# Two index-query projections as one more seven-product pair, with earlier token sums and a one-pass Silu

## The chip, the cores and the metric

The kernel runs on one core of a Trainium2 chip. The metric is the device time of one execution in microseconds. The parts of the core that appear below are TensorE (PE, matrix products; PEld is its loading of weights), VectorE (DVE, elementwise work), ScalarE (ACT, functions and copies), GpSimd (POOL) and SyncE (SP, which issues most loads). Data lies in SBUF (128 partitions); matrix products land in PSUM banks and are taken out by ACT or DVE.

## The reference

One layer of a hybrid encoder on 512 tokens plus 16 learned meta tokens, width 2048, all in float32. The input is normalised and multiplied by one wide matrix whose columns are cut into parts:

```python
h = rms_norm(x, norm_g)
proj = h @ w_in                                   # [528, 2048] @ [2048, 12368]
(q_a, k_a, v_a, z_a, q_i, k_i, w_i,
 q_b, f_b, i_b, z_b, gates) = jnp.split(proj, cuts, axis=-1)
qi = apply_partial_rope(q_i.reshape(B, T, H_IDX, D_IDX), *rope_i)   # 16 heads of 64
...
score = jnp.einsum('bqhs,bqh->bqs', jax.nn.relu(idx_logits), wib)   # token indexer
_, sel = lax.top_k(score, topk)                   # 128 keys for each query
...
y_a = o_a * jax.nn.silu(z_a)                      # attention over the selected keys
y_b = o_b * jax.nn.silu(z_b)                      # gated linear recurrence
merged = jnp.sum(jax.nn.sigmoid(gates) * p, axis=2)
return x + merged @ w_out
```

Three parts matter here: q_i, the 1024 columns of index queries (eight blocks of 128 columns, two heads each), and z_a and z_b, the two gate paths of 1024 columns each that go through silu(z) = z * sigmoid(z).

## The kernel before

**Numbers in two halves.** Each float32 operand is split into a high half (fp32r, by an ACT copy) and a low half (the rest, by a DVE subtraction), and a product is three matmuls: high by high, high by low, low by high. The tokens lie as `hH[k]`, `hL[k]` for k = 0 to 15 (128 channels by 528 tokens each), the weights as `wh`, `wl`, three buffers of each in rotation.

**Plain jobs and pairs.** The projection is a list of jobs (L1794 on). A plain job (`Job`) takes 128 columns of the matrix, 16 blocks of channels, 512 tokens: 48 matmuls of 512 tokens. A `Pair` takes two blocks of 128 columns and computes them with seven products in place of eight (the Winograd form of Strassen's scheme): the channels are cut into two halves of eight blocks, the tokens into two halves of 256 (or 264 with the meta tokens). Its seven products `SEVEN` (L1506) are 24 matmuls each, `run_pair` (L1517) issues them. For the weights a pair needs four sums of raw chunks (`sum_1`, `sum_2` on DVE, `sum_3`, `sum_4` as accumulating DMAs on POOL's queue) and seven splits; for the results it combines the products in four PSUM banks called x, y, z and w (the tiles `px`, `py`, `pz`, `pw`) into two tiles g1 and g2, one for each block of columns. Before, the plain jobs are job 0 (index keys), jobs 1 to 8 (index queries) and jobs 9 and 10 (two blocks of z_b); the pairs follow: three of z_b, four of z_a, then keys with values, queries, gates and the recurrence's inputs, 43 in all. For the plain jobs the low half of a weight chunk is made by an ACT copy with scale -1 and an accumulating DMA (`hi_lo`, L430: preparations 8 to 21).

**Token sums.** The pairs need sums of the tokens' blocks too: `tops_task` (L1462) makes for each k from 0 to 7 the sums t1 and t2 (tile `tT`, high and low halves), t3 (kept in a shared slot until `place_t3`, L1494, writes it over a part of `hH[k]` and `hL[k]` that no later product reads otherwise) and t4 (one more tile `tT`, both halves in it). Two such tasks are spawned ahead of job 3 (`pre_t`, L1783, L1797). The first pair uses t2 in product 1, t3 in product 3, t1 in product 4 and t4 in product 5, counted from 0.

**Index tasks.** When a job of index queries is done, `idx_task` (L677) rotates it (DVE: a shuffle, two products, a sum), splits it into two tiles `qst`, and for each of its two heads issues ten matmuls into `psc`, lets ACT take them out with Relu, and adds them to the four score tiles with DVE. After the eighth of them the top-k tasks begin (`topk_task`, L752); attention needs their result after the last pair.

**Gate paths.** `silu` (L1406) and `silu_mul` (L1348) compute z * sigmoid(z): a Sigmoid on ACT, then a multiplication on DVE into a new slot, which is stored to DRAM by `spill`.

**What sets the order.** The program is written out by hand-made planning: the class `Core` keeps an estimated clock for each engine; `pump` is called after each block of channels and steps waiting tasks in order of their priority (a lower number first), as long as the estimated clocks of DVE and ACT are not too far ahead. A task that yields `WAIT` is asked again later; that moves its instructions in the order of the program. The engines run their queues in that order and wait for each other by semaphores.

**Slots.** SBUF beside the weights is 70 slots of 128 by 528 numbers (`Slots`). A slot's number modulo 4 is its place modulo 256 bytes, and the tiles that PE reads ask for a given residue (`home`). `main_slot` (L1509) steps tasks until a slot is free; `room` holds token tasks back while few are free.

Of the kernel before, what the change touches and what calls it, by code (L numbers as in the profile page):

```python
# [151 lines left out]
class Slots:  # L152
# [40 lines left out]

    def add(self, tags):
# [7 lines left out]
def hybrid_kernel(ctx, tc, x, meta, vecs, w_in, rows, w_branch, w_out,  # L202
# [117 lines left out]
    tabs = slots("tabs", 1)  # L320
    tabA = tabs[0][:, 0:320].rearrange("p (b d) -> p b d", b=5)
    RB = tabs[0][:, 320:512]
# [4 lines left out]
    def load_consts():  # L327
        nc.sync.dma_start(RB, rows.to_broadcast([128, 192]))
# [3 lines left out]
        nc.sync.dma_start(tabA, tab_a)  # L332
# [79 lines left out]
    def hi_lo(k, src, m, o, shift=0, turn=None):  # L412
# [17 lines left out]
        if 8 <= k < 22:  # L430
# [85 lines left out]
    def consts():  # L516
        yield E.clk["pe"] + 3000.0
# [17 lines left out]
        S.put(tabs[0])  # L535
# [85 lines left out]
    def ki_task(kw):  # L621
# [22 lines left out]
        E.tt(y, y, RB[:, None, 0:64].to_broadcast([128, 5, 64]), OP.mult)  # L644
# [30 lines left out]
    idx_left = [8]  # L675

    def idx_task(j, xq):  # L677
        a, b = slot("qpx"), slot("qxc")
# [6 lines left out]
        S.put(a, xq)  # L685
# [5 lines left out]
        S.put(b)  # L691
        yield e
# [6 lines left out]
        for i in range(2):  # L699
# [29 lines left out]
        S.put(*st_)  # L729
        idx_left[0] -= 1  # L730
# [110 lines left out]
    def tokens(src, x, d, tab, name):  # L841
# [12 lines left out]
        yield from room(1, 3)  # L854
# [24 lines left out]
    def ka_task(g, xk):  # L879
        y = yield from tokens({(0, 256): xk[:, 8:264], (2, 256): xk[:, 272:528]}, xk, kd_[g][:, 16:528],  # L880
                              "k", "ka")
        yield from room(1)
# [76 lines left out]
    def q_task(h, xq):  # L959
        y = yield from tokens({(0, 512): xq[:, :512]}, xq, qd_[h], "q", "qa")  # L960
        yield from room(1)
# [410 lines left out]
    def d_qi(j):  # L1372
        def f(b):
            s = slot("xqi")
# [70 lines left out]
    def d_zb(h):  # L1445
        def f(b):
            s = silu_mul(b, "hz")
            hg.setdefault(h, {})["z"] = 1
            spawn(spill(zd[h], s, E.clk["dve"] + LAT), 0)
# [10 lines left out]
    TB = {}  # L1460

    def tops_task(i):  # L1462
# [3 lines left out]
        for k in range(4 * i, 4 * i + 4):  # L1466
            while len(S.free) < (min(10, 6 + idx_left[0]) if idx_left[0] else 6) or k > 3 and k - 4 not in TB:
                yield WAIT
            if k % 2 == 0:
                t3 = slot("t3")  # L1470
            r1, r2, t1 = slots("tr", 3)
            c = r2
            d = t3[:, 264 * (k % 2):264 * (k % 2) + 264]
            E.tt(r1[:, al], hH[k][:, al].bitcast(F32), hL[k][:, al].bitcast(F32), OP.add)
            yield E.tt(r2[:, al], hH[8 + k][:, al].bitcast(F32), hL[8 + k][:, al].bitcast(F32), OP.add)
            E.tt(t1[:, lo], r1[:, lo], r1[:, hi], OP.subtract)
            E.tt(t1[:, hi], t1[:, lo], r2[:, hi], OP.add)
            E.tt(d, r1[:, hi], r2[:, hi], OP.subtract)
            e = E.tt(c[:, lo], r2[:, lo], t1[:, hi], OP.subtract)
            S.put(r1)  # L1480
            yield e
            a, b, t4 = slots("tT", 2, F32R, HC) + [slot("tT", F32R, HD)]
            E.act(a[:, al], t1[:, al], AF.Copy)
            E.act(t4[:, lo], c[:, lo], AF.Copy)
            E.tt(b[:, al], t1[:, al], a[:, al].bitcast(F32), OP.subtract)
            e = E.tt(t4[:, hi], c[:, lo], t4[:, lo].bitcast(F32), OP.subtract)
            S.put(t1, c)
            TB[k] = {"11": (hH[k][:, lo], hL[k][:, lo]), "t3": (hH[k][:, hi], hL[k][:, hi]),
                     "21": (hH[8 + k][:, lo], hL[8 + k][:, lo]), "22": (hH[8 + k][:, hi], hL[8 + k][:, hi]),
                     "t1": (a[:, lo], b[:, lo]), "t2": (a[:, hi], b[:, hi]), "t4": (t4[:, lo], t4[:, hi]),  # L1490
                     "tiles": (a, b, t4), "t3f": d, "t3s": t3}
            yield e

    def place_t3(k):  # L1494
# [4 lines left out]
        h, l = TB[k]["t3"]  # L1499
# [559 lines left out]
```

## Time and profile before

| | |
|---|---|
| median of 3 runs | 1464.0 us (1463.54 to 1464.99) |
| the profiled execution | 1463.6 us, of which 1461.6 us are its span, from the first to the last instruction |
| granted TensorE clock | 1.000 |
| PE busy | 1444.5 us (99%) |
| DVE busy | 1184.5 us (81%) |
| ACT busy | 715.6 us (49%) |
| POOL busy | 271.1 us (19%) |
| DMA | 263.35 MB, mean 180 GB/s |

Times in the profile are counted from the first instruction of the span. The start, with the norm and job 0 and 1, runs to about 50 us; the other plain jobs to 174 us; the pairs to 1081 us; then come the branch products with attention between them, and from 1301 us the last projection. A row of the profile names the line, the engine, the operation, and the tiles (out<-in); a line can be that of a helper, such as L107 for every ACT function and L114 for every DVE operation on two tensors.

### The profile page before, as it was taken

The numbers are of one execution on the slowest core, as the hardware profiler recorded it, in microseconds if no ns is written. First come the engines' busy times: TensorE is split into PE (matmuls) and PEld (weight loads), VectorE is DVE, ScalarE is ACT, GpSimd is POOL, SyncE is SP. The second block draws the span as 40 slices with busy tenths as digits, with TensorE's granted clock in tenths as the row PEclk, the third lists the DMA queues.
The fourth block names the chain that finished last, engine by engine and source line by source line (L and its number), as shares of the span: only waits on it lengthen the run. The fifth ranks groups of instructions, "written<-read, shape, count | busy, mean of one in ns | idle before, by whom it ended". The sixth has DMA issues, their size and how long they took to land.

```text
span 1461.6 us, 33043 instructions
## 1 busy us (share of the span) xinstructions
PE 1444.5 (99%) x13312; PEld 1408.9 (96%) x13312; DVE 1184.5 (81%) x2019; ACT 715.6 (49%) x1172; POOL 271.1 (19%) x346
## 2 busy tenths in 40 slices
PE   7999999999999999999999999999999999999999
PEld 6888899999999999999999999999999999999998
DVE  6699799999999988878877887888675666877676
ACT  5577644543545544444444444444466763334333
POOL 2201000002223310000001011000337410102222
PEclk9999999999999999999999999999999999999999
DMA  9266677778788987778777687868887434458873
GB/s 278 74 157 138 153 182 192 189 185 200 203 205 229 249 196 175 167 173 194 168 191 179 167 195 174 188 143 195 207 267 189 136 111 128 147 143 215 216 210 97
DMA packets 336072, 263.35 MB, mean 180 GB/s; under 512 B 32484, under 2 KB 303408, under 8 KB 335920
## 3 DMA queue, kind: packets, MB, share of 16 engines
q1 hardware_dynamic: 306160, 174.51, 41.9%
q0 software_dynamic: 24256, 80.45, 28.5%
q10 hardware_dynamic: 5504, 6.29, 1.3%
q8 instruction: 104, 1.70, 0.5%
q14 instruction: 48, 0.39, 0.1%
HBM read 170.40 MB, written 29.98 MB: 137 GB/s over the span
## 4 chain that ended last, share of the span: by engine, by line
PE 91%; DVE 4%; DMA 2%; issue 1%; ACT 1%; POOL 0%; SPq 0%; DVEq 0%; ACTq 0%; POOLq 0%
PE px L97 15%; PE pz L97 15%; PE py L97 14%; PE pg L97 12%; PE po L97 10%; PE pg L99 8%; PE pw L97 8%; PE psc L99 1%; PE phl L99 1%; DVE wl L114 1%; PE pov L97 1%; PE plg L99 1%; PE pho L99 1%; PE ppt L103 1%; ACT wh L107 1%
## 5 line engine op out<-in xcount | busy, mean ns | idle before, releaser
L107 ACT ACTIVATE wh<-raw 128x1024 fp32r<-128x1024 f32 x305 | 323.2, 1061 | 454.0 <-PE pz L97 117.6
L114 DVE TENSOR_TENSOR wl<-raw,wh 128x1024 fp32r<-128x1024 f32 (+1 forms) x291 | 357.3, 1229 | 98.0 <-ACT wh L107 96.0
L97 PE MATMUL px<-hH,wh 128*128 128x256 f32 (+1 forms) x688 | 195.0, 284 | 0.0
L97 PE MATMUL px<-hH,wl 128*128 128x256 f32 (+1 forms) x688 | 192.6, 280 | 0.0
L97 PE MATMUL px<-hL,wh 128*128 128x256 f32 (+1 forms) x688 | 192.4, 280 | 0.0
L107 ACT ACTIVATE wh<-sum 128x1024 fp32r<-128x1024 f32 x102 | 108.3, 1062 | 156.7 <-PE pw L97 64.0
L97 PE MATMUL pg<-yH,wh 128*128 128x256 f32 x1024 | 161.6, 280 | 0.0
L97 PE MATMUL po<-wh,mh 128*128 128x256 f32 x896 | 154.4, 277 | 0.0
L114 DVE TENSOR_TENSOR wl<-sum,wh 128x1024 fp32r<-128x1024 f32 x102 | 128.2, 1257 | 26.1 <-ACT wh L107 25.8
L97 PEld LDWEIGHTS pg<-yH,wh 128*128 128x128 f32 x1024 | 136.7, 188 | 0.4
L97 PEld LDWEIGHTS po<-wh,mh 128*128 128x128 f32 x896 | 135.7, 188 | 0.0
L97 PEld LDWEIGHTS px<-hH,wh 128*128 128x128 f32 x688 | 129.6, 188 | 0.6
L97 PEld LDWEIGHTS px<-hL,wh 128*128 128x128 f32 x688 | 129.6, 188 | 0.0
L97 PEld LDWEIGHTS px<-hH,wl 128*128 128x128 f32 x688 | 129.6, 188 | 0.0
L97 PE MATMUL pw<-tT,wh 128*128 128x256 f32 (+1 forms) x688 | 126.5, 284 | 1.5 <-DVE attn L1229 1.5
L97 PE MATMUL po<-wl,mh 128*128 128x256 f32 x448 | 124.5, 278 | 1.8 <-DVE wl L114 1.8
L97 PE MATMUL pz<-tT,wh 128*128 128x256 f32 (+1 forms) x688 | 122.8, 280 | 0.0
L97 PE MATMUL py<-tT,wh 128*128 128x256 f32 (+1 forms) x688 | 122.5, 280 | 0.0
L97 PEld LDWEIGHTS pw<-tT,wh 128*128 128x128 f32 x688 | 105.3, 188 | 2.2 <-PE pz L97 2.0
L97 PEld LDWEIGHTS py<-tT,wh 128*128 128x128 f32 x688 | 104.7, 188 | 0.0
L97 PEld LDWEIGHTS pz<-tT,wh 128*128 128x128 f32 x688 | 104.6, 188 | 0.1
L123 POOL DMA_DIRECT2D raw<-raw x51 | 44.3, 869 | 324.7 <-DVE sum L114 280.8
(316 smaller groups left out, 3799.0 us busy)
## 6 DMA issues: line engine op xcount, KB each, us to landing
raw<-in_w_in_dram SPq DMA_DIRECT2D x192, 512.0 KB, 4.5
raw<-raw POOLq DMA_DIRECT2D x51, 512.0 KB, 5.3
raw<-sum POOLq DMA_DIRECT2D x51, 512.0 KB, 5.3
raw<-in_w_branch_dram SPq DMA_DIRECT2D x32, 512.0 KB, 4.9
raw<-in_w_out_dram SPq DMA_DIRECT2D x32, 512.0 KB, 4.5
gd<-g SPq DMA_DIRECT2D x32, 256.0 KB, 4.7
g<-gd POOLq DMA_DIRECT2D x30, 256.0 KB, 3.2
wl<-raw POOLq DMA_DIRECT2D x14, 512.0 KB, 4.5
```

The source lines that it names most:

```text
L97: self.nc.tensor.matmul(out, lhsT, rhs, start=start, stop=stop, skip_group_check=True)
L99: self.nc.tensor.matmul(out, lhsT, rhs, start=start, stop=stop)
L103: self.nc.tensor.transpose(out, in_, ident)
L107: self.nc.scalar.activation(out, in_, f, **kw)
L114: self.nc.vector.tensor_tensor(out, a, b, op=op)
L123: self.nc.gpsimd.dma_start(out, a, accum_op=OP.add)
```

## The change

**Jobs.** Index queries 0 to 5 stay plain jobs; 6 and 7 become one pair, the first of now 44. Its two results go to `idx_task` without a copy (`d_qp`). Preparations 8 to 17 in place of 8 to 21 make their low half by DMA, which are again the plain jobs.

**Index tasks.** They work in the tile that they get, begin their rotation in the order of the jobs, and yield when there are no slots: two free for the split if no other index task holds one, seven otherwise.

**Token sums.** `tops_task` is spawned ahead of job 2 with the priority of the index tasks, and starts a k with four free slots (before: six, and up to ten while index tasks are open). t3 and t4 stay in one tile v. t3 is placed in the second half of the last plain job where its k is ready, otherwise as before; t4 is made by `place_t4` in product 3 of the first pair.

**Silu.** z_a and z_b use ScalarE's Silu, in place where they come from a pair. (q_b keeps Sigmoid and a multiplication.)

**Small things.** The tables for keys and queries are loaded by `consts`, ahead of the third z_a pair, and hold a slot only from then on; the index key's gain is loaded into free columns of CQ. Token tasks wait for two spare slots where they waited for three or four. `again` is a new method of `Slots` that nothing calls.

```diff
 class Slots:
+    def again(self, a, name, dt):
+        ...
     def load_consts():
-        nc.sync.dma_start(RB, rows.to_broadcast([128, 192]))
+        nc.sync.dma_start(CQ[:, 512:576], rows[:, 0:64].to_broadcast([128, 64]))
...
-        nc.sync.dma_start(tabA, tab_a)
     def hi_lo(...):
-        if 8 <= k < 22:
+        if 8 <= k < 18:
     def consts():
-        yield E.clk["pe"] + 3000.0
+        while not S.free:
+            yield WAIT
+        tabs = slot("tabs")
+        tabA = tabs[:, 0:320].rearrange("p (b d) -> p b d", b=5)
+        RB = tabs[:, 320:512]
+        nc.sync.dma_start(RB, rows.to_broadcast([128, 192]))
+        nc.sync.dma_start(tabA, tab_a)
+        yield E.clk["pe"] + 6000.0
     def idx_task(j, xq):
-        a, b = slot("qpx"), slot("qxc")
+        while not S.free or idx_on[0] < j:
+            yield WAIT
+        a, b = slot("qpx"), xq
...
+        while len(S.free) < (2 if not idx_on[1] else 7):
+            yield WAIT
         st_ = slots("qst", 2, F32R)
+        idx_on[1] += 1
...
+                while not S.free:
+                    yield WAIT
                 r = slot("rl")
     def tokens / ka_task / q_task:
-        yield from room(1, 3)    /    room(1)
+        yield from room(1, 2)    /    room(1, 2)
     def d_qi(j):
-            s = slot("xqi")
+            s = main_slot("xqi")
+    def d_qp(j):
+        return lambda x: spawn(idx_task(j, x), 1)
     def d_za(h):
-            s, e = silu(g, "zs")
-            spawn(spill(zad[h], s, e), 0)
+            spawn(spill(zad[h], g, E.act(g[:, :512], g[:, :512], AF.Silu)), 0)
     def d_zb(h):
-            s = silu_mul(b, "hz")
+            s = slot("hz")
+            E.act(s[:, :512], b, AF.Silu)
+            B1.put(b)
     def d_zp(h):
-            s, e = silu(g, "hz")
-            spawn(spill(zd[h], s, e), 0)
+            spawn(spill(zd[h], g, E.act(g[:, :512], g[:, :512], AF.Silu)), 0)
     def tops_task(i):
-            while len(S.free) < (min(10, 6 + idx_left[0]) if idx_left[0] else 6) or k > 3 and k - 4 not in TB:
+            while len(S.free) < 4 or k > 3 and k - 4 not in TB:
                 yield WAIT
-            if k % 2 == 0:
-                t3 = slot("t3")
-            r1, r2, t1 = slots("tr", 3)
...
+            u, v, t = slots("tr", 3)
+            E.tt(u[:, al], hH[k][:, al].bitcast(F32), hL[k][:, al].bitcast(F32), OP.add)
+            yield E.tt(v[:, al], hH[8 + k][:, al].bitcast(F32), hL[8 + k][:, al].bitcast(F32), OP.add)
+            E.tt(t[:, lo], u[:, lo], u[:, hi], OP.subtract)
+            E.tt(t[:, hi], t[:, lo], v[:, hi], OP.add)
+            E.tt(v[:, hi], u[:, hi], v[:, hi], OP.subtract)
+            e = E.tt(v[:, lo], v[:, lo], t[:, hi], OP.subtract)
+            S.put(u)
+            yield e
+            while len(S.free) < 2:
+                yield WAIT
+            a, b = slots("tT", 2, F32R, HC)
...
+    def place_t4(k):
+        while not S.free:
+            pump(1e9)
+            if not S.free:
+                E.clk["pe"] += 200
+        t, c = slot("tT", F32R, HD), TB[k]["v"]
+        E.act(t[:, 0:264], c[:, 0:264], AF.Copy)
+        E.tt(t[:, 264:528], c[:, 0:264], t[:, 0:264].bitcast(F32), OP.subtract)
+        S.put(c)
+        TB[k]["t4"] = (t[:, 0:264], t[:, 264:528])
+        TB[k]["tiles"].append(t)
     def run_pair(pr, nxt, late, last):
-                if pr is pairs[0] and i == 1:
+                if pr is pairs[0] and i == 1 and k not in placed:
                     place_t3(k)
+                if pr is pairs[0] and i == 3:
+                    place_t4(k)
     def pre_t():
-        t_task.extend(spawn(tops_task(i), 2) for i in range(2))
+        t_task.extend(spawn(tops_task(i), 1) for i in range(2))
-    jobs += [Job("in", C_QI + 128 * j, 128, done=d_qi(j)) for j in range(8)]
+    jobs += [Job("in", C_QI + 128 * j, 128, done=d_qi(j)) for j in range(6)]
-    jobs[3].pre = pre_t
+    jobs[2].pre = pre_t
+    for j in range(6, 8, 2):
+        two(*((C_QI + 128 * i, d_qp(i)) for i in (j, j + 1)))
     # the loop over the plain jobs
+                if job is plain[-1] and kt > 7 and kt - 8 in TB:
+                    place_t3(kt - 8)
                 pump()
```

More of the change, by code (lines that the diff above doesn't have):

```diff
@@ L192, in put @@
             self.free.append(t)
+    def again(self, a, name, dt):
+        nm = a.tensor.name
+        t = self.tag.pop(nm)
+        self.k += 1
+        b = self.pool.tile(self.shape, dt, name=f"{name}_{self.k}", tag=t)
+        self.tag[b.tensor.name] = t
+        self.core.ac[b.tensor.name] = self.core.ac[nm]
+        return b
     def add(self, tags):
@@ L853, in tokens @@
         yield E.clk["pe"] + 9000.0
-        yield from room(1, 3)
+        yield from room(1, 2)
         sq = slot(name + "s")
@@ L881, in ka_task @@
                               "k", "ka")
-        yield from room(1)
+        yield from room(1, 2)
         tb = slot("kT")
@@ L960, in q_task @@
         y = yield from tokens({(0, 512): xq[:, :512]}, xq, qd_[h], "q", "qa")
-        yield from room(1)
+        yield from room(1, 2)
         tb = slot("qT")
@@ L1446, in f @@
         def f(b):
-            s = silu_mul(b, "hz")
+            s = slot("hz")
+            E.act(s[:, :512], b, AF.Silu)
+            B1.put(b)
             hg.setdefault(h, {})["z"] = 1
-            spawn(spill(zd[h], s, E.clk["dve"] + LAT), 0)
+            spawn(spill(zd[h], s, E.clk["act"] + LAT), 0)
         return f
@@ L1453, in f @@
         def f(g):
-            s, e = silu(g, "hz")
             hg.setdefault(h, {})["z"] = 1
-            spawn(spill(zd[h], s, e), 0)
+            spawn(spill(zd[h], g, E.act(g[:, :512], g[:, :512], AF.Silu)), 0)
         return f
-    TB = {}
+    TB, placed = {}, []
     def tops_task(i):
@@ L1475, in tops_task @@
[L1475 to L1480, printed above, removed]
-            yield e
-            a, b, t4 = slots("tT", 2, F32R, HC) + [slot("tT", F32R, HD)]
-            E.act(a[:, al], t1[:, al], AF.Copy)
@@ L1488, in tops_task @@
+            E.tt(t[:, hi], t[:, lo], v[:, hi], OP.add)
+            E.tt(v[:, hi], u[:, hi], v[:, hi], OP.subtract)
+            e = E.tt(v[:, lo], v[:, lo], t[:, hi], OP.subtract)
+            S.put(u)
+            yield e
+            while len(S.free) < 2:
+                yield WAIT
+            a, b = slots("tT", 2, F32R, HC)
+            E.act(a[:, al], t[:, al], AF.Copy)
+            e = E.tt(b[:, al], t[:, al], a[:, al].bitcast(F32), OP.subtract)
+            S.put(t)
             TB[k] = {"11": (hH[k][:, lo], hL[k][:, lo]), "t3": (hH[k][:, hi], hL[k][:, hi]),
@@ L1489, in tops_task @@
                      "21": (hH[8 + k][:, lo], hL[8 + k][:, lo]), "22": (hH[8 + k][:, hi], hL[8 + k][:, hi]),
-                     "t1": (a[:, lo], b[:, lo]), "t2": (a[:, hi], b[:, hi]), "t4": (t4[:, lo], t4[:, hi]),
-                     "tiles": (a, b, t4), "t3f": d, "t3s": t3}
+                     "t1": (a[:, lo], b[:, lo]), "t2": (a[:, hi], b[:, hi]),
+                     "tiles": [a, b], "v": v}
             yield e
@@ L1498, in place_t3 @@
                 E.clk["pe"] += 200
-        h, l = TB[k]["t3"]
-        E.act(h, TB[k]["t3f"], AF.Copy)
-        E.tt(l, TB[k]["t3f"], h.bitcast(F32), OP.subtract)
-        if k % 2:
-            S.put(TB[k]["t3s"])
+        (h, l), d = TB[k]["t3"], TB[k]["v"][:, 264:528]
+        E.act(h, d, AF.Copy)
+        E.tt(l, d, h.bitcast(F32), OP.subtract)
+        placed.append(k)
+    def place_t4(k):
[9 more added lines that the diff above has]
+        TB[k]["tiles"].append(t)
     SEVEN = (("11", "11", "x", 0), ("s2", "t2", "y", 0), ("12", "21", "x", 1), ("s3", "t3", "y", 1),
@@ L1794, in hybrid_kernel @@
     jobs = [Job("in", C_KI, 80, True, done=d_kiwi)]
-    jobs += [Job("in", C_QI + 128 * j, 128, done=d_qi(j)) for j in range(8)]
+    jobs += [Job("in", C_QI + 128 * j, 128, done=d_qi(j)) for j in range(6)]
     jobs += [Job("in", C_ZB + 128 * h, 128, done=d_zb(h)) for h in range(NZ)]
-    jobs[3].pre = pre_t
+    jobs[2].pre = pre_t
     jobs[-1].pre = lambda: (sum_1(jobs[ji]), sum_2(jobs[ji]), hold.append(1))
+    plain = list(jobs)
     def two(a, b, **kw):
```

19 lines of the change are left out of this document (6 added, 13 removed).

## The prediction

> **What bounds the kernel now.** The page comes first, then the table of stretches, then PE's waits.
>
> ```profile
> span 1461.6 us, 33043 instructions
> PE 1444.5 (99%) x13312; PEld 1408.9 (96%) x13312; DVE 1184.5 (81%) x2019; ACT 715.6 (49%) x1172; POOL 271.1 (19%) x346
> PE 91%; DVE 4%; DMA 2%; issue 1%; ACT 1%; POOL 0%; SPq 0%; DVEq 0%; ACTq 0%; POOLq 0%
> ```
>
> PE is busy 99% of the span and is 91% of the chain that ended last. The next fence is the table of stretches: length, then busy time of PE, PEld, DVE, ACT and POOL with instruction counts, granted clock, DMA share, GB/s. The stretches are the plain jobs, the first pair, the six pairs after it, and the pairs up to the recurrence.
>
> ```profile
> 49.26:174.46 125.20, 125.20 (x623) 105.20 (x621) 103.70 (x203) 82.79 (x138) 16.84 (x19) 1.00 0.61 141
> 174.46:193.97 19.51, 19.51 (x171) 19.36 (x170) 17.49 (x34) 10.90 (x19) 1.70 (x2) 1.00 0.66 152
> 193.97:310.12 116.15, 116.15 (x1010) 116.15 (x1010) 112.65 (x225) 56.79 (x70) 10.19 (x12) 1.00 0.81 192
> 310.12:553.42 243.30, 242.23 (x2055) 241.38 (x2054) 222.97 (x380) 116.41 (x226) 62.83 (x88) 1.00 0.86 211
> ```
>
> PE has no gap in the first three, although DVE is busy for 112.65 of 116.15 us in the third. The waits of PE over the whole span (total us, times, longest) say the same; each row with 1 us or more is here.
>
> ```profile
> PE pc L103 <- DMA vrow<-in_vecs_dram: 7.7, 1, 7.7
> PE po L97 <- DVE wl L114: 1.8, 3, 0.9
> PE pw L97 <- DVE attn L1229: 1.5, 3, 0.5
> PE pz L97 <- DVE g L114: 1.1, 3, 0.4
> ```
>
> The first is the load before any work, and the change does not touch it. The others together are 4.4 us. So the time is the number of matmuls times their spacing, and an engine beside PE can only cost. What PE spends on each job is read from the chain of waits in order of time (start, length, work), around the end of the plain jobs and over the first two pairs:
>
> ```profile
> 161.94 1.33 PE psc L99 x10
> 163.27 11.19 PE pg L99 x48
> 174.46 2.75 PE px L97 x24
> 177.21 2.74 PE py L97 x24
> 179.95 2.74 PE px L97 x24
> 182.69 2.96 PE py L97 x24
> ...
> 188.38 2.85 PE pw L97 x24
> ...
> 193.97 2.74 PE px L97 x24
> ...
> 202.19 2.82 PE py L97 x24
> ...
> 210.60 2.73 PE pz L97 x24
> 213.33 1.71 PE px L97 x15
> ```
>
> A plain job of 128 columns is 48 matmuls of 512 tokens in 11.19 us, 233 ns each. A pair does two such jobs in 168 matmuls of 256 columns. The second pair runs from 193.97 to 213.33: 19.36 us, 115 ns each.
>
> **The change, part by part.** *Jobs 6 and 7 of the index query as a pair.* Out go 2 x 11.19 = 22.38 us of PE; in comes one pair, at the 19.36 us of an undisturbed one. That is -3.02 us. The new pair's matmuls are of a known form; if they all ran at the dearest product in the quoted rows, 2.96, the pair would be 20.72 and the gain 1.66; at the cheapest, 2.73, it would be 19.11 and 3.27. I take 19.36, since the operands and shapes are the same. By the Trainium skill (TensorE: Matmul & The Clock Gate, section Back-to-back issue gap), a warm matmul takes N/2.4 + 2.5 ns, so 96 of 512 against 168 of 256 columns would be an estimated gain of 2.4 us; the trace differs, with 233 ns where that rule has 216, and the measurement decides.
>
> The score matmuls (psc, 1.33 us a head) stay 16 heads; four of them move behind the first pair. At 1.33 there as well they cost nothing more.
>
> *The split parts.* Four of the DMA additions that make low halves of plain jobs go, and DVE makes seven for the new pair, with two sums of raw chunks and five small combinations. Two raw additions on POOL's queue come with the pair. All this lies beside PE, where each pair's set of the same work already does without a gap.
>
> The new `WAIT` loops act while the program is written: on the chip they add no wait, they set where instructions stand in the queues.
>
> *The token sums.* `tops_task` starts at plain job 2 and not 3, but two plain jobs fewer follow. It now holds u, v, t and two result slots; t4 is made later. Its last piece ends close ahead of its use: the last tT is at 173.05 (DVE's timeline), and the product that needs it starts at 177.21.
>
> ```profile
> 173.05 1.05 DVE L114 TENSOR_TENSOR tT<-tr,tT 128x528 fp32r<-128x528 f32 x2
> ```
>
> Will DVE be through in time? First by sum, from the plain stretch: the tiles score, qxc and the two lines of qpx (each by busy us and count) are the work of the eight index tasks.
>
> ```profile
> 49.26:174.46 125.20, 32.12 (x64) 1.00 0.61 141
> 49.26:174.46 125.20, 21.91 (x32) 10.03 (x16) 1.00 0.61 141
> L681 DVE STREAM_SHUFFLE qpx<-xqi 128x512 f32<-128x512 f32 x8 | 5.9, 739 | 0.0
> L114 DVE TENSOR_TENSOR qpx<-qpx,sq 128x512 f32<-128x512 f32 x8 | 5.5, 685 | 0.0
> ```
>
> That is 65.4 us, 8.2 a task. Of the 103.7 us of DVE work, 16.4 (two tasks) and 3.4 (t4, eight pieces at the 0.43 of the last row below) move behind the pair's start, 0.7 (one Silu product) goes, and 2.8 (t3, now in the second half of the last plain job) comes in: 86.0 us. The time up to the first use is 125.2 - 22.4 - 4 x 1.33 + 2.75 = 100.2 us. DVE fits with 14 us to spare. No PE cost is taken; the bound above is with the rivals.
>
> *t3 and t4.* In the first pair t3 is made inside product 1 (DVE 2.83, ACT 2.62 us for eight, second row below), and the product that reads it takes 2.96 in place of 2.82. With most of t3 made in the last plain job this 0.14 us goes. t4 is made inside product 3 for product 5, one product of distance as t3 had: the same 0 to 0.14 us could come back; I take 0, since only the eviction of pz lies between. The last row is the present t4.
>
> ```profile
> 174.46:193.97 19.51, 2.83 (x8) 2.62 (x8) 1.00 0.66 152
> L114 DVE TENSOR_TENSOR tT<-tr,tT 128x264 fp32r<-128x264 f32 x8 | 3.4, 427 | 0.0
> 189.84 0.41 DVE L114 TENSOR_TENSOR g<-p,pz 128x256 f32<-128x256 f32 x1
> ```
>
> *Two index tasks inside the pairs.* 16.4 us of DVE goes into pairs 1 to 3, which have 19.36 us each. DVE runs late there already: the eviction g<-p,pz above starts at 189.84, 1.46 us after pz ended (188.38 by the chain, the start of pw). Pw, 2.85 us, is all the time that eviction has before the next pz overwrites its bank. The three waits on g (1.1 us) are that deadline missed; they fall behind 310 (the fourth stretch lacks 1.07 us of PE), where the token tasks of keys and queries run at the priority of the index tasks. Below: the eviction is ahead of time, 0. Above: each of the two tasks holds its first score matmul by DVE's lateness, 2 x 1.46, and three evictions miss by 0.4, in all 4.1 us. The trace has 1.1 us for twelve token tasks; two tasks at that price are 0.2, which I take. Top-k starts later and fills what is left; nothing reads it before attention, after the last pair.
>
> *Silu.* ScalarE's function is exchanged, and DVE's product goes: 8 and 6 in pairs (two rows, 9.6 us) and, by the code, two in plain jobs at 0.68. That is some 11 us of DVE, in stretches where PE never waits for it: 0. Silu has no row. From below it is a Sigmoid (third row, 0.62); from above it loads a table before and after each (fourth row), 3.2 us each or 45 for 14. ACT is idle for 59 of 116 us there, so this too is hidden; I take the Sigmoid's price. If the cover were gone, the first to be late would be the copy p<-px, which has one product, 2.74 us.
>
> ```profile
> L114 DVE TENSOR_TENSOR zs<-g,zs 128x512 f32<-128x512 f32 x8 | 5.5, 684 | 0.0
> L114 DVE TENSOR_TENSOR hz<-g,hz 128x512 f32<-128x512 f32 x6 | 4.1, 684 | 0.0
> L107 ACT ACTIVATE zs<-g 128x512 f32<-128x512 f32 x8 | 5.0, 621 | 0.0
> L107 ACT ACT_TABLE_LOAD x5 | 6.4, 1283 | 1.0 <-PEq L2046 0.7 <-DVE score L135 0.2
> ```
>
> *Constants.* Two small loads go from SP's queue during the start to the pairs of z_a. Behind them in that queue stand raw chunks, loaded six ahead; nothing waits: 0. The relaxed `room` limits let token tasks begin earlier; they add no work.
>
> *Sum.* -3.02 - 0.14 + 0.2 = -2.96 us. The profiled execution took 1463.6 us around its span of 1461.6, so 1460.6 for it; the median shown is 1464.0, 0.4 above, so 1461.0. A measurement of this kernel can tell about 0.2%, 2.9 us: the forecast lies just on that line, at 1461.07.
>
> **The rivals.** *More than the sum (B).* The planner is run anew; the waits on g (1.1 us) could vanish with 11 us less DVE work: -3.02 - 0.14 - 1.1 gives 1459.7. For: DVE is the only engine that ever stops PE in the pairs. Against: those waits stand behind the Silu pairs, and top-k is pushed towards them.
>
> *The index tasks collide (C).* The upper 4.1 us in place of 0.2: 1464.9. For: the lateness of 1.46 us. Against: six pairs at 97% DVE without one wait.
>
> *The spacing of the plain matmuls is not their width (D).* The 233 ns might belong to the traffic of that stretch, so that the removed matmuls are worth less; the gain is then no more than the lower bound 1.66 + 0.14: 1462.4. For: a product of the same form varies from 2.73 to 2.96. Against: 2 x 115 is close to 233 in any case. The 2.4 us of the Trainium skill's rule lies between this and my sum.
>
> *Token sums too late (E), slower.* Place: product 1 of the new pair, whose PE loop waits for t2 of each k. In the plain stretch DVE was idle for 125.2 - 103.7 = 21.5 us. If the index tasks, queued on few free slots, make all of that idle time again, DVE needs 86.0 + 21.5 = 107.5 us where there are 100.2: 7.3 us late, and the time is 1468.3. It decides from 17.2 us of idle time, where the lateness passes the 2.96 of the sum. Against: the thresholds of free slots that held the sums back are lowered, and two tasks may move behind.
>
> *Slots in other places (F).* t4 takes any free slot late in the first pair. Pw takes 0.11 us more than px now; if badly placed t4 doubles that in 44 pairs, it is +4.8 us: 1465.8. Against: t4 still asks for its own residue.
>
> **How the numbers follow.** Forecast 0.58, B 0.16, C 0.07, D 0.06, E 0.09, F 0.04. Predicted is the forecast, 1461.0. Its own range runs from 1460.6 (a pair of the cheapest products, no late eviction) to 1461.9 (0.14 back at t4, and half of one 1.46); 1461.07 cuts it: 0.30 faster, 0.28 the same. Faster: 0.30 + 0.16 = 0.46. Slower by over 2.9 us (above 1466.9): 0.07 of E and 0.02 of F, 0.09. The same: 0.45. The range is 1459.6 to 1465.2: it takes in B, the forecast, D and C and leaves out E and most of F, with a little below B.
>
> **What would show it.** Right: 44 pairs in the profile, the plain stretch shorter by 22.4 us and four heads, a first pair with no product over 2.9 us but for a psc between, later pairs of 19.36 us, and PE's waits with no new row above 0.5 us. ACT_TABLE_LOAD x6 or so, DVE's mean lateness at g<-p,pz under 2.85 us. Wrong: a PE row that waits for tT or hL (E), for qst or g in pairs 1 to 3 (C), pw above 2.85 in every pair (F), or plain jobs that now run at another spacing than 11.19 us (D).

## The result and the profile after

The changed kernel takes 1473.08 us (median; 1472.24 to 1475.46) beside 1463.83 us for the kernel before on the same chip: ratio 1.0066, 95% interval 1.0053 to 1.0079. It became slower by 9.3 us where 3.0 us of gain was forecast. Its profiled execution took 1472.37 us around a span of 1470.6 us. From its page, the span, the busy times and the engines' shares of the chain that ended last:

```profile
span 1470.6 us, 33183 instructions
PE 1446.4 (98%) x13384; PEld 1413.1 (96%) x13384; DVE 1188.7 (81%) x2017; ACT 715.5 (49%) x1172; POOL 270.7 (18%) x344
PE 88%; DMA 4%; DVE 4%; ACT 2%; issue 1%; POOL 1%; SPq 0%; ACTq 0%; DVEq 0%; POOLq 0%
```

TensorE (PE) is busy 1.9 us more than before, where 3.0 less was forecast, and VectorE (DVE) 4.2 us more; in the chain, transfers grow from 2% to 4%. PE's waits (total us, times, longest) have new rows:

```profile
PE pc L103 <- DMA vrow<-in_vecs_dram: 7.8, 1, 7.8
PE px L97 <- ACT p L107: 2.9, 2, 2.0
PE pz L97 <- DVE g L114: 2.6, 3, 1.3
...
PE psc L99 <- ACT g L107: 1.0, 1, 1.0
```

The new waits come to some 6 us, and the time is 12 above the forecast. Where the loss lies is read from the starts of the pairs, each the first px matmul of a pair in the trace. There are 44 pairs now, counted from 0; pair 0 is the new one, and pair j is pair j-1 of the kernel before. The table gives what each stretch takes more than in the kernel before (us), in the profiled executions. The first column runs from the span's start to pair 3, less PE's wait for the very first load (pc above, 7.36 to 8.82 us in these executions), which no edit touches. Each line is one execution, the profiled one; it can lie some microseconds from the median beside it (e7: 1470.58 for 1466.58).

| kernel | to pair 3 | pairs 3-12 | pairs 13-19 | pairs 20-43 | median us |
|---|---|---|---|---|---|
| changed | -0.21 | -0.54 | +7.31 | +2.37 | 1473.08 |
| e1 room limits back | -0.28 | -0.63 | +6.92 | +1.50 | 1472.68 |
| e3 jobs plain again | +0.82 | +1.32 | +2.28 | +0.11 | 1467.62 |
| e4 loads by ScalarE | -0.29 | -0.58 | +8.24 | +0.72 | 1475.24 |
| e5 tokens used later | -0.13 | -0.53 | +4.55 | +1.51 | 1471.02 |
| e6 masks early | -0.22 | -0.25 | +0.01 | +1.66 | 1465.45 |
| e7 shorter lead | +0.03 | -0.62 | +5.57 | +1.78 | 1466.58 |
| e10 e6, stores by ScalarE | -0.32 | +0.65 | +20.96 | +2.67 | 1488.84 |
| e11 e6, later copies | -0.56 | -0.40 | +1.43 | +0.77 | 1465.89 |
| e12 e10 and e11 | -0.57 | +5.47 | +12.04 | +2.74 | 1483.22 |
| e13 one index task later | -0.69 | -0.10 | +11.16 | +1.40 | 1477.35 |
| e14 e6 and e13 | -0.60 | -0.28 | +0.05 | +0.03 | 1462.78 |
| e15 e14 and e5 | -0.59 | -0.39 | +3.92 | +1.42 | 1470.46 |
| e16 e11 (with e6) and e13 | -1.94 | -0.36 | +1.56 | +1.92 | 1464.66 |
| before + e2 room limits | -0.13 | -0.21 | -0.45 | 0.00 | 1464.31 |
| before + e8 Silu | -0.21 | +3.74 | +3.37 | 0.00 | 1469.74 |
| before + e9 masks early | -0.22 | +5.45 | +4.28 | 0.00 | 1473.43 |

Three things happened to the changed kernel. Of the 3.17 us that should stand at pair 3 (3.02, and 0.15 that the kernel before's first pair, 19.51, took above 19.36) 0.21 was left; 7.3 us were lost in pairs 13 to 19, whose matmuls the change does not touch, 4.69 of them in pair 17 and 1.23 in pair 13; and 2.4 us in pairs 20 to 43, nearly all of it in pairs 27 and 39. The table of stretches, first over pairs 0 to 2 and then over parts of pair 17 (columns as in the prediction):

```profile
144.85:167.37 22.52, 22.36 (x189) 21.91 (x188) 19.59 (x33) 13.78 (x24) 1.70 (x2) 1.00 0.57 129
167.37:191.07 23.70, 22.66 (x191) 22.11 (x189) 21.64 (x33) 13.32 (x19) 1.70 (x2) 1.00 0.61 143
191.07:213.14 22.07, 22.07 (x191) 22.07 (x190) 21.54 (x41) 11.90 (x17) 1.70 (x2) 1.00 0.69 159
...
491.09:496.40 5.31, 5.31 (x49) 5.31 (x48) 3.69 (x8) 1.30 (x3) 0.92 (x1) 1.00 0.75 206
496.40:498.70 2.30, 0.33 (x3) 0.12 (x2) 0.28 (x1) 2.30 (x11) 0.00 (x0) 1.00 1.13 344
498.70:502.00 3.30, 3.29 (x15) 3.30 (x16) 3.30 (x6) 0.90 (x1) 2.15 (x4) 0.50 0.42 103
```

Each of pairs 0 to 2 holds two heads of scores, 2.64 us beside 19.36, so 22.00. Pair 0 takes 22.69 by the starts, pair 1 23.70, pair 2 22.07: 2.46 us lost (the first matmul of pair 0 stands at 144.68; the row begins a little later). Another 0.50 is lost ahead of pair 0, which without loss would begin at 174.30 - 22.38 - 6 x 1.32 = 144.00, with 0.18 more for the first load. It lies in one head of scores, 1.88 us from 124.78 where the others take 1.32: its bank is taken out late by ScalarE, behind a weight half. The chain there:

```profile
123.36 1.07 ACT wh L107
...
125.41 0.60 ACT rl L107
...
126.06 0.76 PE psc L99 x4
```

Pair 1's loss is in ScalarE's timeline:

```profile
175.25 1.29 ACT L107 ACTIVATE qst<-g 64x512 fp32r<-64x512 f32 x2 [1.20 <-DVE g L114]
176.57 1.06 ACT L107 ACTIVATE wh<-raw 128x1024 fp32r<-128x1024 f32 x1
177.53 0.37 ACT L107 ACTIVATE g<-px 128x256 f32<-128x256 f32 x1
```

ScalarE takes its instructions in their order. It stands 1.20 us before the copy of an index task whose rotation VectorE has not ended; behind the copy stand a weight half and the eviction g<-px, which holds the bank that the scores want. In pair 17 the same happens with a transfer. ScalarE's timeline:

```profile
496.16 0.31 ACT L107 ACTIVATE qas<-qay 128x128 f32<-128x128 f32 x1 [3.88 <-DMA qay<-qd]
...
498.29 0.36 ACT L107 ACTIVATE p<-px 128x256 f32<-128x256 f32 x1
```

The chain of waits over the same place:

```profile
493.50 2.59 DMA qay<-qd
...
497.44 0.95 ACT wh L107
498.38 0.28 ACT p L107
...
498.70 4.61 PE px L97 x24
```

ScalarE stands 3.88 us before a token load, the eviction p<-px comes late behind it, PE is idle for about 2.0 us (0.33 busy of the 2.30 in the stretch above), and the next product takes 4.61 us, since the clock granted for the following 3.3 us is 0.50 (the row before it has 1.00). Idle 2.0, half clock about 1.65 (half of 3.30) and a second small gap of 0.6 (after 504) are 4.25 of the 4.69 us that pair 17 lost. The load was issued late: SyncE's own timeline (start, length, queue, issue) around it is

```profile
452.44 25.53 SPq L399 DMA_DIRECT2D raw<-in_w_in_dram  x6
478.03 3.50 SPq L827 DMA_DIRECT2D qd<-qT  x4
...
493.50 0.34 SPq L874 DMA_DIRECT2D qay<-qd  x1
```

and in the kernel before

```profile
462.89 3.57 SPq L394 DMA_DIRECT2D raw<-in_w_in_dram  x2
466.51 3.60 SPq L805 DMA_DIRECT2D qd<-qT  x4
...
479.83 0.35 SPq L852 DMA_DIRECT2D qay<-qd  x1
```

The stores come 11.5 us later and the load 13.7. In the rows left out between them twelve more stores stand ahead of that load, eight in the kernel before, and one load of raw chunks for two. Pair 13 (+1.23) lost its time in another queue; the chain there:

```profile
411.48 0.63 DVE qat L817
...
412.39 1.35 POOL qd L827 x3
...
414.58 8.92 DMA raw<-sum
...
427.35 0.43 DVE g L114
...
427.91 3.15 PE pz L97 x24
```

On GpSimd's (POOL) queue the turned tokens' stores stand ahead of the accumulating transfer of sum_4, wait for VectorE's qat, and the transfer lands 8.92 us after its issue. PE waits 1.3 us there, at a granted clock of 1.00 behind it. That the stores make the transfer late is read from this chain and from the same chain in e8; no run tests it by itself.

### The profile page after: what moved, and what is told of

The parts are those of the page before. It is cut to its first block, busy times and chain, and to the rows that moved or that the text cites. A ratio compares the mean times of both kernels' runs of the same rounds, so it can differ in the third digit from the quotient of the medians.

```text
span 1470.6 us, 33183 instructions
## 1 busy us (share of the span) xinstructions
PE 1446.4 (98%) x13384; PEld 1413.1 (96%) x13384; DVE 1188.7 (81%) x2017; ACT 715.5 (49%) x1172; POOL 270.7 (18%) x344
## 4 chain that ended last, share of the span: by engine, by line
PE 88%; DMA 4%; DVE 4%; ACT 2%; issue 1%; POOL 1%; SPq 0%; ACTq 0%; DVEq 0%; POOLq 0%
PE px L97 16%; PE pz L97 14%; PE py L97 14%; PE pg L97 12%; PE po L97 9%; PE pw L97 8%; PE pg L99 6%; DMA raw<-sum 2%; PE psc L99 1%; DMA raw<-in_w_in_dram 1%; DVE wl L114 1%; PE phl L99 1%; PE pov L97 1%; ACT wh L107 1%; PE plg L99 1%
## 5 line engine op out<-in xcount | busy, mean ns | idle before, releaser
L114 DVE TENSOR_TENSOR wl<-raw,wh 128x1024 fp32r<-128x1024 f32 (+1 forms) x296 | 362.3, 1226 | 107.4 <-ACT wh L107 104.9
L97 PE MATMUL px<-hH,wh 128*128 128x256 f32 (+1 forms) x704 | 200.3, 285 | 3.3 <-ACT p L107 2.9
L97 PE MATMUL px<-hH,wl 128*128 128x256 f32 (+1 forms) x704 | 197.5, 281 | 0.0
L97 PE MATMUL px<-hL,wh 128*128 128x256 f32 (+1 forms) x704 | 197.3, 280 | 0.0
L114 DVE TENSOR_TENSOR wl<-sum,wh 128x1024 fp32r<-128x1024 f32 x104 | 132.6, 1275 | 25.8 <-ACT wh L107 25.6
L97 PEld LDWEIGHTS px<-hH,wh 128*128 128x128 f32 x704 | 133.4, 190 | 4.5 <-ACT p L107 3.3
L97 PEld LDWEIGHTS px<-hL,wh 128*128 128x128 f32 x704 | 133.4, 189 | 0.0
L97 PEld LDWEIGHTS px<-hH,wl 128*128 128x128 f32 x704 | 133.2, 189 | 0.0
L97 PE MATMUL pw<-tT,wh 128*128 128x256 f32 (+1 forms) x704 | 129.8, 285 | 1.7 <-DVE attn L1251 1.5
L97 PE MATMUL py<-tT,wh 128*128 128x256 f32 (+1 forms) x704 | 125.9, 280 | 0.1
```

What stands on the lines that cost most here:

```text
L97: self.nc.tensor.matmul(out, lhsT, rhs, start=start, stop=stop, skip_group_check=True)
L114: self.nc.vector.tensor_tensor(out, a, b, op=op)
```

## The experiments

Unless it is said otherwise an edit computes the same; "e6 and e13" means that the edits stand together. The letters of the theories are those of each expectation.

**e1, e2: the room limits.** In the changed kernel the old limits, in the kernel before the new ones:

```diff
-        yield from room(1, 2)      # e1, at the three places; e2 the other way
+        yield from room(1, 3)      # in tokens; room(1) in ka_task and q_task
```

> The changed kernel with the three limits of free slots for the token tasks as they were (3, 4 and 4 spare slots, not 2). The changed kernel loses 6.9 us between its pairs 10 and 19, the token tasks' time. Theory R: the lower limits let these tasks run closer together, and their small DMAs crowd SP's and POOL's queues; then this run is without most of the 6.9: 1466 to 1468 us, with no pair there over 2 us longer than before. Rival N: the limits don't matter, the loss comes from the new order of everything behind the first pair; then it stays above 1471.

> The kernel before with the lower limits (2 spare slots) alone. Theory R: slower by 3 to 7 us (1467 to 1471), the loss in the pairs between 330 and 550 us. Rival N: within 1 us of 1463.8.

e1: 1472.68 us, ratio to the kernel before 1.0060 (1.0045 to 1.0075), pair 17 at 24.53. e2: 1464.31, ratio 1.0003 (0.9993 to 1.0012). Rival N in both: the limits are neither the cause nor of a price that is clear of the noise.

**e3: the two jobs plain again**, all else as in the changed kernel.

```diff
-        if 8 <= k < 18:
+        if 8 <= k < 22:
-    jobs += [Job("in", C_QI + 128 * j, 128, done=d_qi(j)) for j in range(6)]
+    jobs += [Job("in", C_QI + 128 * j, 128, done=d_qi(j)) for j in range(8)]
-    for j in range(6, 8, 2):
-        two(*((C_QI + 128 * i, d_qp(i)) for i in (j, j + 1)))
```

> The changed kernel with index queries 6 and 7 as plain jobs again; all else changed. By PE's matmuls alone it is 3.0 us more. Theory C (the two index tasks inside the pairs collide with the evictions, 2.5 us in the first two pairs): these 2.5 go, so the first part comes out as before, within 0.7. Theory R: the 6.9 us in the middle stay: 1471 to 1474 in all. Rival N (the pair's shift makes the loss in the middle): back to 1464 to 1466.

1467.62 us, ratio 1.0027 (1.0017 to 1.0037), between rival N's band and theory R's: pairs 13 to 19 lose 2.28 us in place of 7.31. So the other edits cost 3.8 us without the pair, and the pair, worth -3.0 by its matmuls, adds 5.5. The late head of scores ahead of the first pair is here too (1.86 us), so it is not the pair's.

**e4: the token loads by ScalarE's queue**, so that they do not stand behind SyncE's stores.

```diff
-        nc.sync.dma_start(y[:, :512], d)
+        nc.scalar.dma_start(y[:, :512], d)
```

> The changed kernel with one edit that leaves the order of all engines' work alone: the load of a token task's tile (qay<-qd, kay<-kd) is issued by ScalarE's queue in place of SP's. Theory L: in pair 17 ScalarE stood 3.9 us before a tile whose load had been issued late behind small stores on SP's queue; PE waited 2.2 us and ran at half clock for 3.3 us after it. Then this run has no such gap and is 4 to 4.7 us faster: 1468 to 1469. Rival: the load is late for another reason (the DMA engines are full), ScalarE waits as long: 1472 to 1475.

1475.24 us, ratio 1.0081 (1.0049 to 1.0112); pair 17 still 23.81. From PE's waits over the whole span:

```profile
PE pz L97 <- DVE g L114: 3.2, 3, 1.8
...
PE px L97 <- ACT p L107: 0.6, 1, 0.6
```

The wait for p fell from 2.0 to 0.6, as theory L had it. But in the same pair another came up: an accumulating transfer that GpSimd issued behind token stores at 503.55 landed 5.98 us later, PE waited 1.8 us for g, and the product behind it took 4.58. So the place of the load's issue explains its own wait and not the loss of the pair.

**e5: the tokens used later.**

```diff
         nc.sync.dma_start(y[:, :512], d)
-        yield E.clk["pe"] + 9000.0
+        yield E.clk["pe"] + 14000.0
```

> The changed kernel, but the planner takes 14 us instead of 9 for the load of the turned tokens, so that their norm is written some 5 us later into ScalarE's and VectorE's queues; nothing is computed otherwise. Theory N (in pair 17, counted from 0, ScalarE stands 3.88 us before a load that lands late, TensorE idles 2.25 us behind it and then runs 3.3 us at half clock): pair 17 falls from 24.05 to 19.4 to 20.0, and the time from 1473.1 to 1467.5 to 1469.5. Rival M (the stretch has too much work on VectorE and the DMA engines, wherever ScalarE stands): the stall moves to pairs 18 to 20 or the token tasks hold their slots longer, and the time stays at 1471.5 to 1474.

1471.02 us, ratio 1.0052 (1.0036 to 1.0069). Pair 17 falls to 21.75 and pair 13 from 22.14 to 20.42, but pair 16 rises from 19.90 to 21.84. The loss is cut and moved, between the two expectations.

**e6: the masks early.** In the changed kernel SyncE issues the masks' load at 414.58, ahead of a token load at 415.38; in the kernel before the token load stands first (409.44, masks 415.10).

```diff
-        if g == 2:
+        if h == 6:                      # in the loop of the z_a pairs
             jobs[-1].pre = lambda: spawn(make_masks(), 2)
```

> The changed kernel, but the masks are loaded and made during the last pair of z_a, six pairs before the place they have; nothing is computed otherwise. Theory N's upstream half (the masks' load overtook a token load on SyncE, whence three token tasks came to VectorE together and their stores in one clump): the token tasks spread out again, pair 17 falls to 19.4 to 20.5, the time to 1468 to 1470. Rival M (the clump comes from the index tasks and token tasks that are all late): pair 17 stays at 23 to 24.5, the time at 1472 to 1474.

1465.45 us, ratio 1.0015 (1.0005 to 1.0024), below what was expected. The table of stretches over pair 17:

```profile
489.93:509.40 19.47, 19.47 (x172) 19.47 (x171) 17.68 (x30) 9.15 (x17) 7.26 (x11) 1.00 1.02 254
```

No gap and the full clock. Pairs 13 to 19 take what they took before (+0.01), 7.3 us less than in the changed kernel. That much hung on the order of the work alone, since the edit adds none and takes none away.

**e7: a shorter lead in the first pairs.**

```diff
-                pump(1500.0 if i in (0, 1, 4) and k > 2 else 3000.0)
+                pump(1500.0 if i in (0, 1, 4) and k > 2 or pr in pairs[:3] else 3000.0)
```

> The changed kernel, but in the first three pairs the planner lets VectorE and ScalarE be at most 1.5 us of work ahead of TensorE, not 3; nothing is computed otherwise. Theory C (the index tasks' pieces stand in front of the pairs' evictions): pairs 0 to 2, now 22.69, 23.70 and 22.07 for 58.08 of products and 7.92 of scores, lose 1 to 2.4 us; pair 3 starts that much earlier. Rival W (the first pairs have more work on VectorE than they last): the same sum of pairs 0 to 2 within 0.5 us, perhaps in another place. What follows after pair 10 is planned anew and is read apart from this; the time is 1468 to 1475 by either.

1466.58 us, ratio 1.0023 (1.0012 to 1.0034), but up to pair 3 nothing is gained (+0.03), which is rival W's reading in words. What the median gained must lie behind, in the new order; the profile does not show it, since its execution was the slowest of this kernel, 1470.58: in it VectorE stands before the masks in pair 13, whose load takes 9.03 us to land, and PE waits 3.4 us for p.

**e8: Silu alone**, on the kernel before.

```diff
-            s, e = silu(g, "zs")
-            spawn(spill(zad[h], s, e), 0)
+            spawn(spill(zad[h], g, E.act(g[:, :512], g[:, :512], AF.Silu)), 0)
```

(and Silu in place of Sigmoid and product in d_zp and d_zb)

> The kernel before with nothing of the change but Silu: ScalarE applies Silu, VectorE's product is gone. Theory: Silu itself costs nothing (0.62 us as Sigmoid had), the pairs of z stay at 19.36; the planner's order behind them moves, and the time is 1463 to 1466. Rival T (a table is loaded around each Silu, 1.28 us each, and p<-px is late behind it): the pairs of z get 0.5 us or more each, in all 4 or more, 1467 to 1470.

1469.74 us, ratio 1.0041 (1.0026 to 1.0056). An edit that takes work away from VectorE and gives ScalarE one load of a table (1.28 us) costs 5.9 us. 3.40 us of its loss are in one pair, the changed kernel's number 10 (23.46 in place of 20.06): not in the Silu pairs, of which one takes 0.36 more and the others what they took. The time is in rival T's band, but rival T falls: its place was the Silu pairs. The chain in pair 10:

```profile
352.85 0.72 DVE qat L795
...
356.03 9.16 DMA raw<-sum
...
369.03 0.34 DVE g L114
...
369.51 4.60 PE pz L97 x24
```

It is the mechanism of pair 13 above: qat, the stores, the accumulating transfer, a late eviction, and a product of 4.60 us, with a granted clock of 0.57 from 370.00 to 373.94.

**e9: the masks early in the kernel before**, with e6's edit.

> The kernel before, with the masks loaded and made during the last pair of z_a, as in the run with early masks; nothing is computed otherwise. Theory O (what the early masks healed is the changed kernel's order, where their load overtook a token load; the kernel before has that order right already): 1463 to 1465. Rival G (masks in the token stretch cost every kernel about the same, so the changed kernel's 7.6 us were not its own): 1456 to 1461. Rival R (every edit of the plan shifts what stands behind it and costs some microseconds, as Silu alone did): 1466 to 1470, with the loss in one or two pairs between 9 and 18.

1473.43 us, ratio 1.0067 (1.0055 to 1.0080): theory R's kind of loss, beyond its 1470 and with one of the two large losses in an earlier pair (7; the other is in pair 16). What healed the changed kernel costs the kernel before 9.4 us. VectorE's waits over the pair that has the masks now (23.73 for 19.36) and, in the second fence, its stretches:

```profile
DVE masks L339 <- DMA mf<-in_masks_dram: 3.4, 1, 3.4
```

```profile
304.00:306.00 2.00, 0.49 (x5) 0.29 (x3) 1.93 (x5) 1.06 (x1) 0.00 (x0) 1.00 0.00 0
306.00:308.00 2.00, 0.91 (x7) 0.91 (x8) 2.00 (x4) 0.00 (x0) 0.00 (x0) 0.99 0.89 246
308.00:310.00 2.00, 2.00 (x12) 2.00 (x11) 2.00 (x4) 0.00 (x0) 0.85 (x1) 0.50 0.24 43
```

VectorE stands 3.4 us before a transfer, PE idles behind it, and the clock falls to 0.50. So early masks are not good in themselves; they gave the changed kernel an order that fits.

**e10: e6, and the turned tokens stored by ScalarE's queue.** PE, VectorE and SyncE keep e6's order.

```diff
-        fan(d, tb, 4, nc.gpsimd)
+        fan(d, tb, 4, nc.scalar)
```

> The changed kernel with early masks, and the turned tokens go to memory by ScalarE's queue, not GpSimd's; TensorE's, VectorE's and SyncE's instructions stay in the same order as with early masks alone, and nothing is computed otherwise. Theory P (on GpSimd's queue these stores, 0.67 us each and held until VectorE has turned the tokens, stand before the accumulating transfer of a pair's fourth sum, which then lands late): pairs 10, 13 and 18, now 19.54, 21.29 and 20.76, lose 0.5 to 2 us together, and the time goes from 1465.45 to 1463.5 to 1465. Rival A (ScalarE, which evicts p<-px in order, stands before these stores instead): 1465.5 to 1468.

1488.84 us, ratio 1.0173 (1.0158 to 1.0187). Both theories fell; the cost is far beyond rival A's. ScalarE's timeline in pair 13 (27.47 us):

```profile
414.10 4.60 ACTq L827 DMA_DIRECT2D kd<-kat  x4
418.79 2.49 ACTq L827 DMA_DIRECT2D qd<-qat  x4
421.38 1.06 ACT L107 ACTIVATE wh<-sum 128x1024 fp32r<-128x1024 f32 x1 [6.98 <-DMA qd<-qat]
```

Issuing eight of these stores holds ScalarE for 7 us, with every eviction and weight half behind them; PE then waits 4.2 us for g. VectorE had turned these tokens by 412.1 (kat) and 414.1 (the first qat), so the stores were not held for it. Whether another queue than GpSimd's would help is therefore not settled by this run.

**e11: e6, and the last three index tasks' copies later.**

```diff
         S.put(a)
-        yield e
+        yield e + (3000.0 if j > 4 else 0.0)
```

> The changed kernel with early masks, and for the last three index tasks the planner takes VectorE's rotation to end 3 us later, so that the copies qst<-g are written later into ScalarE's queue; nothing is computed otherwise. Theory C (in pair 1 ScalarE stands 1.20 us before qst<-g, and the eviction g<-px behind it holds the bank of the scores: 1.31 us of gap): pair 1 falls from 23.72 to 22.0 to 22.6, pair 3 starts at 211.8 to 212.6 in place of 213.32. Rival W (VectorE's work in these pairs is the bound, wherever it stands): pair 3 starts within 0.4 us of 213.32. The order behind is planned anew: 1463 to 1468 by either.

1465.89 us, ratio 1.0017 (1.0008 to 1.0026). PE's waits over pairs 0 to 2:

```profile
PE pw L97 <- DVE p L114: 1.2, 1, 1.2
PE pw L97 <- ACT wh L107: 0.2, 1, 0.2
```

The wait psc<-g is gone, and p, an eviction on VectorE behind the eighth task's rotation, takes its place: pair 1 23.56, pair 3 at 213.02, where rival W had it.

**e12: e10 and e11 together.**

> The changed kernel with early masks, the later copies of the last three index tasks, and the turned tokens by ScalarE's queue; nothing is computed otherwise. If the pair's arithmetic (3.02 us) is real and only the order ate it, a kernel that has these three mended comes below the kernel before: 1461 to 1463.5. If every change of the plan brings a loss of its own elsewhere (theory R): 1465 to 1469.

1483.22 us, ratio 1.0138 (1.0121 to 1.0156), above both expectations; e10's stores again. It tells nothing on the pair.

**e13, e14, e15: the eighth index task later**, on the changed kernel; with e6; with e6 and e5.

```diff
     def idx_task(j, xq):
+        if j > 5:
+            yield E.clk["pe"] + 20000.0 * (j - 6)
```

> The changed kernel, but the eighth index task begins some 20 us later, at the end of pair 1 and not in its middle; nothing is computed otherwise. Theory W (VectorE is busy 21.64 of pair 1's 23.70 us, and TensorE's own work there is 22.0: two index tasks and a pair's sums are more than the pair holds): pair 1 falls from 23.70 to 21.4 to 22.3, pair 3 starts at 211.4 to 212.4 in place of 213.14. Rival C (what collides is one task's pieces with one eviction, at any density): pair 3 starts within 0.4 us of 213.14. Theory R (whatever is moved, the token tasks behind are ordered anew, for better or worse by 2 to 9 us): the end is anywhere from 1463 to 1475, and pairs 10 to 20 say where.

> The changed kernel with early masks and the eighth index task 20 us later; nothing is computed otherwise. Early masks alone took 1465.45. If the gain in pairs 0 to 2 comes through and the order behind stays near that of early masks: 1463 to 1464.5, level with the kernel before. If the order behind is lost again (theory R): 1466 to 1475.

> As the run before it, and the turned tokens' load taken as 14 us, so that their norm is written later. In the changed kernel this took pair 13 from 22.14 to 20.42 and put 2 us into pairs 16 and 17 each. If the two mend different pairs: 1462 to 1464. If the order behind is lost again (theory R): 1466 to 1475.

e13: 1477.35 us, ratio 1.0094 (1.0079 to 1.0110); pair 3 starts at 213.04, within rival C's 0.4 us. VectorE's work in pair 1 falls from 21.64 to 20.79 us and the pair still takes 23.43, so W's forecast fails; what settles it is e16 below. Pair 13 takes 28.77. e14: 1462.78 us, ratio 0.9995 (0.9986 to 1.0004), level with the kernel before and the best order found; its pairs 13 to 43 cost +0.08 in the profiled execution. e15: 1470.46 us, ratio 1.0042 (1.0028 to 1.0055): e5's edit takes pair 13 from 21.81 to 20.91, as in the changed kernel, and puts more into pairs 17 (21.45 for 19.35) and 19 (22.26 for 20.30).

**e16: e6, e11 and e13 together.**

> The changed kernel with early masks, the eighth index task 20 us later, and the copies qst<-g of the last three index tasks 3 us later in the plan; nothing is computed otherwise. Taken singly, the later copies moved pair 1's stall to an eviction behind the eighth task's rotation, and the later task left the copies' stall in place; together neither should be left. Theory CC (two collisions stand one behind the other, each covering the other): pair 1 falls from 23.5 to 22.0 to 22.3 and pair 3 starts at 211.2 to 211.8 in place of 212.82. Rival W (VectorE's sum of work): pair 3 starts within 0.4 us of 212.82. If the order behind stays as good as in the run with both masks and spread (1462.78): 1461 to 1462; if it is lost again: 1466 to 1475.

1464.66 us, ratio 1.0008 (0.9999 to 1.0017). PE's waits over pairs 0 to 2, whole:

```profile
PE pw L97 <- ACT wh L107: 0.2, 1, 0.2
```

Pair 1 is 22.20, as theory CC expected: two collisions stood one behind the other. VectorE is busy 60.5 us over pairs 0 to 2 here and 60.7 in e14, and the three pairs take 66.9 us for 68.2; so its sum of work is not the cause. Pair 3 starts at 212.38 and not at 211.8 or less, because this execution's first load came 0.9 us later than e14's (8.8 for 7.9); less that, 1.94 of the 3.17 us reach pair 3. Behind it 3.1 us go again in the order.

## Why the prediction was wrong

**The pair's arithmetic, -3.02: right in size.** The pairs without an index task take 19.34 to 19.36 as forecast, and in e16, with the two collisions of pair 1 out, 1.94 us of 3.17 stand at pair 3. The other 1.23 are placed: pair 0 (0.69, of which 0.40 is t4's, below), pair 1 (0.21) and the time ahead of pair 0 (0.33).

**t3 and t4, -0.14: the wrong way.** Counted from first matmul to first matmul, the product that reads t3 and the one ahead of it take 2.83 and 2.72 us in pair 0, for 2.82 and 2.88 in the first pair of the kernel before, so the 0.14 went. But products 4 and 5 take 5.98 us for 5.58: ScalarE makes the weight half that product 5 needs behind its copies of t4, and PE stands before it. That is +0.40, above the bound of 0.14, and not by the path that was looked at (the reading of t4) but by what stands behind its making in ScalarE's queue. It also breaks the forecast's own sign of a first pair with no product over 2.9. From the chain of the changed kernel, with a later pw beside it (t4's row in the prediction is the second of its three, not the last):

```profile
158.16 1.81 DVE tT L114 x5
...
160.00 0.37 ACT tT L107
...
160.68 1.05 ACT wh L107
161.73 3.08 PE pw L97 x24
...
185.62 2.85 PE pw L97 x24
```

**Index tasks in the pairs, +0.2: mis-sized.** About 2.1 us in pairs 0 to 2 (2.46 less t4's 0.40), inside the upper bound of 4.1; the 0.50 ahead of pair 0, a head of scores in the plain jobs, had no term at all. That is rival C's place and nearly its price, but not its mechanism: no g<-p,pz missed its deadline there; ScalarE stood before qst<-g, and with that wait gone (e11) VectorE's rotation stood before p. Also six heads moved behind the start of pair 0, not four.

**Silu, constants, room limits, split parts, 0: the step that failed.** "They add no work" was true, and ScalarE's cover was there: ACT_TABLE_LOAD is x6 (7.7 us) for x5 (6.4), and the pairs of z without an index task keep 19.34 to 19.35. What the step put at nothing is the order: an edit changes the planner's clock, and with it the order in the queues a hundred microseconds and more behind. The time lost there is 9.1 us (pairs 3 to 43 of the table), and a move of the masks' load, which has no work at all, takes 7.6 of the 9.3 us away again (e6). The same holds on the kernel before: Silu alone costs 5.9 us (e8), the masks' move alone 9.4 (e9); the room limits alone cost nothing clear of the noise (e2), and the constants and the split parts had no run of their own. The pair has part in it too: pairs 3 to 43 lose 9.1 us with it and 3.7 without (e3). The prediction said that the planner is run anew, and counted it only as a rival's gain (B, -1.1 us for the waits on g); these waits grew from 1.1 to 2.6. A loss from the order behind the first pairs had no rival, no price and no chance. The trace before had signs of it, though no price: token stores and accumulating transfers in one queue, in a stretch where GpSimd is busy 62.83 of 243.30 us after 10.19 of 116.15.

**The other rivals.** D: the plain matmuls' spacing stayed, 21 matmuls in 4.90 us (233 ns). E: no wait for tT, and for hL only the 0.2 us in the start that was there before. F: pw is 2.85 in the later pairs. All three fell. The range's upper end, 1465.2, came from C alone; the reshuffled orders of the changed kernel that kept ScalarE free of the token stores ran from 1462.8 to 1477.4.

**What stays open.** Why one accumulating transfer in each of pairs 27 and 39 takes 6.4 and 6.3 us from issue to landing in the changed kernel and 4.4 in the kernel before, with ScalarE's and GpSimd's instructions in the same order there; the pairs lose 1.04 and 1.23 us by it. e14 lost nothing in pairs 20 to 43 in sum and e16 1.9; no run separated the cause. Pairs 15, 18 and 19 lost 0.3 to 0.6 us each, which was not followed up. Whether an order exists that keeps the whole 3 us was not found: e14 is level, and no kernel here beat the one before by more than its interval.

## What to carry to other kernels

Where a program plans its own queues and engines take them in order, the price of an edit is its work plus the order that it leaves behind, and the second can be larger: here -3 us of work against orders that cost -0.2 to +12.5 us (pairs 3 to 43 of the table, the changed kernel and the runs on it, without e10 and e12). Before forecasting a small gain, list the places where an in-order engine stands close ahead of a transfer's landing, and price one of them missed (here some 2 us of idle, and 1.7 more where the clock halves behind it). Then test an edit with a second, work-free change of the plan before its own worth is judged.

## What the runs showed of the hardware

A gap of about 2 us on PE can be followed by half clock, or not. In pair 17 above PE is idle for 2.0 us, and the granted clock is then 0.50 for 3.4 us in all (its row shows 3.30 of them). Over all runs of this case, between 60 us and the last pair, the gaps of PE sort like this: up to 1.76 us none was followed by a lower clock (the 1.0 us in pair 1 and the 1.3 in pair 13 among them); of the eleven from 1.80 to 2.98 us six were (the changed kernel, e1, e4, e8, e9, e13) and five were not (2.98 us in e9 and 2.83 in e12 among them); the seven from 3.30 us on all were. The slow stretch was 3.4 us long each time but after the three longest gaps, where it was 6 us and more. The Trainium skill (TensorE: Matmul & The Clock Gate, Part 1: The HAM clock gate) speaks of an idle window of about 3.4 us before half rate. Here a shorter idle time was enough six times in eleven, and the measurement decides; what decides between the eleven no run here shows. The length of the slow stretch agrees with the page's 3.4 us.

A DMA issue on ScalarE's queue held it: four stores of turned tokens took 4.60 us in one place and 2.49 in another, and from the eviction at 414.03 to the weight half at 421.38 no activation ran (e10). Four such stores took GpSimd 2.2 to 2.6 us in the changed kernel's pair 13.
